# First quarter of a hybrid decoder trunk: a written start for embedding and first x, embeddings of quarter 1 moved behind the mixers, and delayed steps of the first heads

## The chip, the cores and the metric

The kernel runs on one core of a Trainium2 chip. The metric is the time of one execution on the device in microseconds (us), the median of several runs. The core has a matrix engine (TensorE, PE in the profile; its weight loads are PEld), a vector engine (VectorE, DVE), a scalar engine (ScalarE, ACT), GpSimd (POOL) and a queue engine (SyncE, SP), from which this kernel issues nearly all its DMA transfers. Each engine takes its own instructions in order, and semaphores tie them together.

## The reference

One layer of a decoder with 2048 tokens and 1024 channels, all in float32. Cut to what matters:

```
hn   = rms_norm(x, pre_mix_norm)
proj = hn @ w_in                                 # q,k,v,z,a,b of 4 DeltaNet heads; f,i,q,g of 4 HGRN2 heads
q, k, v = split(silu(causal_conv4(proj_qkv)))
o_a  = gated_delta_rule(l2norm(q), l2norm(k), v, decay(a), sigmoid(b)) -> head norm * silu(z)
o_b  = hgrn2(silu(q_hg), (1-lb)*sigmoid(-f), i_hg, log_f)              -> head norm * silu(g)
h = x + rms_norm(concat(o_a, o_b) @ w_out, post_mix_norm)
h = h + rms_norm(square(relu(rms_norm(h) @ w_up)) @ w_down)
e = rms_norm(p @ w_ple, ple_norm)
out = h + e * sigmoid(h @ w_gate)
```

The change touches the start (the scale of the first x, and p @ w_ple), the order of the two mixers in the first 512 tokens, and the end of the mixers' stage.

## The kernel before

Tokens are worked in four quarters of 512 (`QT`), channels as eight tiles of 128 (`KD`). A float32 product is made of three matmuls of a rounded high part and a low remainder: `split` (line 159) lets ACT write the high part and DVE subtract to get the low one; `operand` (197) does so for a 128x512 tile, after a scaling by a column and a row `rsb` where these are given; `project` (190) issues the three matmuls for each 128 channels. A tile of p @ w_ple has 256 input channels and so 6 matmuls; a block of `w_in` has 1024 and 24 matmuls.

**The start** (349 to 394). SP issues the loads in written order: half of `w_ple`, p of quarter 0, x of quarter 0 by rows (`xs`), small constants, p of quarter 1, the other half of `w_ple`, and x of quarter 0 again, transposed (`xraw`). ACT sums the squares of `xs` (375), POOL takes the power -1/2 (`rsqrt`, 157), and the 512 factors go through DRAM and back to a tile that holds them on all partitions (`spread` 228, `spread_load` 234). PE meanwhile makes 16 tiles of p @ w_ple, quarters 0 and 1 (`embed_tile`, 292): ACT copies each from PSUM and squares it, DVE adds the squares up, and the copy is stored to DRAM (`ed`). Then each of the eight x tiles is scaled and split (392). All this lives in a pool `es`; the mixers' pools `mp` and `m2` take the same room afterwards.

**The mixers' stage** (397 to 978). `works` (799) is a list of 4 x 33 products: for each quarter the decay columns (`mm_ab`) and, for each of four head pairs h, the eight blocks k, q, v, z (DeltaNet) and f, i, q, g (HGRN2). Each product is issued in three thirds of 8 matmuls, and after each third `tick` (344) advances a clock and runs the generators that are due: a head pair takes 24 ticks, a quarter 99. Head pair h of quarter 0 begins at tick t = 3 + 24 h.

`gdn_mixer` (534) is a generator of 39 steps whose offsets from t are `A_STEPS` (50). Counted from 0: step 2 transposes k, step 4 makes the matrices `u` and `qk`, steps 6 to 13 solve 32 rows of small triangular systems on DVE (`pr`, `xs_g`, lines 615 and 616), step 14 (offset 24) stores the result to DRAM, step 15 (26) loads it into `xx`, step 16 (28) transposes it on DVE, step 17 (30) begins the products on `xx` (`psp`, 638), steps 21 to 32 are the recurrence over four chunks (psa, `r` on DVE, psb, `w` on ACT, psc), step 33 on is the head norm. `hgrn_mixer` (681) and `turn_i` (782) have offsets of their own. `u`, `xx` and other tiles have one buffer, k and q (`conv_silu`, tags kT and qT) two.

PE's order is the written one throughout, and so is SP's in these stages; DVE, ACT and POOL are ordered by a planner, which goes by the written order and by which operands its model has ready.

**The end of the stage** (935 to 978). When the last product is issued, the last head pair still has some 20 ticks to go. In these, PE makes the 16 tiles of p @ w_ple of quarters 2 and 3 (one for each tick), whose p operands were loaded ahead (937), and then the first two blocks of the output product (`first_outs`, 949), 8 matmuls a tick. `mix_operands(0)` (313) loads and splits the mixers' result of quarter 0 meanwhile.

Of the kernel before, what the change touches and what calls it, by code (L numbers as in the profile page):

```python
# [20 lines left out]
P = 128  # L21
# [22 lines left out]
N_CONST = C_MASK + 2 * len(LEVELS)  # L44
# [16 lines left out]

def constants():
    j = np.arange(P)[:, None]
    i = np.arange(P)[None, :]
    c = np.zeros((P, N_CONST, P), np.float32)
    c[:, C_IDENT] = (i == j)
    c[:, C_NEG] = np.where(j <= i, 0.0, -1e30)
    c[:, C_UNIT] = (i % SB == GC * (j % GR) + i // SB)
    for n, s in enumerate(LEVELS):

        i = np.concatenate([m * P + np.arange(P).reshape(-1, 2, s)[:, 1].reshape(-1) for m in range(NC)])[None, :]
        m = (j // (2 * s) == i % P // (2 * s)) & (j % (2 * s) < s) | (s == 1) & (j == i % P)
        c[:, C_MASK + 2 * n : C_MASK + 2 * n + 2] = m.reshape(P, 2, P)
    return c
# [3 lines left out]
def trunk(ctx, tc, x, xT, pT, vecs, w_in, w_ab, gdn_a_log, gdn_dt_bias, w_out, w_up, w_down,  # L78
# [30 lines left out]
    mask = [cst[:, C_MASK + 2 * n : C_MASK + 2 * n + 2, :].rearrange("p a b -> p (a b)") for n in range(len(LEVELS))]  # L109
# [20 lines left out]
    def vectors():  # L130

        ps = bank("ps_rows", pp)
        PE.transpose(ps[:, :N_ROWS], rows, ident[:N_ROWS, :N_ROWS])
        V.tensor_copy(cols, ps[:, :N_ROWS])
        V.tensor_scalar(gate_w, cols[:, R_GNORM : R_HNORM + 1], 0.5, None, ALU.mult)
# [141 lines left out]
    def stage_ple(i, name):  # L277
# [5 lines left out]
        def ready(eng):  # L283
            w = wp.tile([P, 2, KD, P], F32R, tag="whl", name=f"w_{name}")
            for half in range(2):
                sl = slice(half * KD // 2, (half + 1) * KD // 2)
                split(w[:, :, sl], eng, raw[:, sl])
            return w
# [15 lines left out]
    x_r, xts, accs = {}, {0: []}, {0: None, 1: None}  # L304
# [44 lines left out]
    with ExitStack() as ectx:  # L349
        es = ectx.enter_context(tc.tile_pool(name="es", bufs=1))  # L350
        with tc.manual_schedule(engines={mybir.EngineType.SP}):
            ple0 = stage_ple(0, "plea0")
            praw = [es.tile([P, 2, QT], F32, name=f"praw{q}") for q in range(2)]
            nc.sync.dma_start(praw[0], pT[:, tok(0)].rearrange("(k p) t -> p k t", p=P))
            rows4 = x[tok(0), :].rearrange("(p c) d -> p c d", c=NC)
            xs = es.tile([P, NC, D], F32, name="xs")
            for c in range(0, NC, 2):
                nc.sync.dma_start(xs[:, c : c + 2], rows4[:, c : c + 2])
            nc.sync.dma_start(ident, consts[:, C_IDENT])
            nc.sync.dma_start(rows, vecs)  # L360
            nc.sync.dma_start(dec[:, 0:1], gdn_a_log.rearrange("o h -> h o"))
            nc.sync.dma_start(dec[:, 1:2], gdn_dt_bias.rearrange("o h -> h o"))
            nc.sync.dma_start(praw[1], pT[:, tok(1)].rearrange("(k p) t -> p k t", p=P))
            ple1 = stage_ple(1, "plea1")
# [6 lines left out]
            ple = [ple0(V), None]  # L371
            pts = [[operand(ra, None, f"pT{q}_{k}", raw=praw[q][:, k]) for k in range(2)] for q in range(1)]
            ss = sm.tile([P, NC], F32, tag="ss", name="ss_x0")
            for c in range(NC):
                S.activation(xs[:, c], xs[:, c], AF.Square, accum_out=ss[:, c : c + 1])
            V.tensor_scalar(ss, ss, 1.0 / D, EPS, ALU.mult, ALU.add)
            rsqrt(ss)
            stores = []
            for d in range(4):
                stores.append(embed_tile(0, d, ple[0], pts[0], accs, es, 6))  # L380
                if d == 1:
                    vectors()
            pts.append([operand(ra, None, f"pT1_{k}", raw=praw[1][:, k]) for k in range(2)])
            ple[1] = ple1(V)
# [1255 lines left out]
```

## Time and profile before

| | us |
|---|---|
| median of 3 runs | 2870.23 |
| lowest, highest | 2867.57, 2871.44 |
| profiled execution, its own time | 2865.62 |
| span of the profiled execution, first to last instruction | 2863.8 |
| PE busy in the span | 2773.0 (97%) |
| DVE busy | 2158.2 (75%) |
| ACT busy | 1331.2 (46%) |

The profile lists for each instruction its line, its tiles (out<-in), its start and length, and what ended the idle time of its engine before it. "x24" means 24 instructions merged in one row. Times inside the profile count from the first instruction. The granted clock (PEclk) is the share of full speed at which the matrix engine was allowed to run.

### The profile page before, as it was taken

The numbers are of one execution on the slowest core, as the hardware profiler recorded it, in microseconds if no ns is written. First come the engines' busy times: TensorE is split into PE (matmuls) and PEld (weight loads), VectorE is DVE, ScalarE is ACT, GpSimd is POOL, SyncE is SP. The second block draws the span as 40 slices with busy tenths as digits, with TensorE's granted clock in tenths as the row PEclk, the third lists the DMA queues.
The fourth block names the chain that finished last, engine by engine and source line by source line (L and its number), as shares of the span: only waits on it lengthen the run. The fifth ranks groups of instructions, "written<-read, shape, count | busy, mean of one in ns | idle before, by whom it ended". The sixth has DMA issues, their size and how long they took to land.

```text
span 2863.8 us, 39544 instructions
## 1 busy us (share of the span) xinstructions
PE 2773.0 (97%) x13361; PEld 2293.7 (80%) x13361; DVE 2158.2 (75%) x4712; ACT 1331.2 (46%) x2460; POOL 108.7 (4%) x104
## 2 busy tenths in 40 slices
PE   7899999999999999999989999999999999999999
PEld 5688788888888888777768887888888888887887
DVE  6688787887878887758887886776787765567675
ACT  6354334333333333457555655554555445465431
POOL 0000000000000000000000000000100000001000
PEclk9999999999999999999999999999999999999999
DMA  7666667655665666587755646666564446577573
GB/s 254 223 222 205 215 213 246 201 199 201 224 195 190 212 199 196 159 284 247 258 173 192 229 166 209 217 212 210 193 210 139 148 157 213 188 255 239 196 230 116
DMA packets 268602, 589.70 MB, mean 206 GB/s; under 512 B 55642, under 2 KB 59960, under 8 KB 249072
## 3 DMA queue, kind: packets, MB, share of 16 engines
q1 hardware_dynamic: 268400, 587.18, 61.5%
q8 instruction: 106, 1.74, 0.3%
q14 instruction: 96, 0.79, 0.1%
HBM read 420.14 MB, written 166.92 MB: 205 GB/s over the span
## 4 chain that ended last, share of the span: by engine, by line
PE 46%; DVE 3%; DMA 3%; issue 2%; ACT 2%; POOL 0%; SPq 0%; DVEq 0%; ACTq 0%; POOLq 0%
PE u L996 21%; PE d L996 18%; PE mmg L996 6%; DMA da<-sumd 1%; DMA raw_out<-in_w_out_dram 1%; DMA xo<-in_xT_dram 1%; DMA b<-h1d 0%; PE mmo L996 0%; DVE w_out L162 0%; DVE t L162 0%; ACT L1033 0%; ACT L1032 0%; ACT w_out L161 0%; DVE b L1143 0%; POOL acc_y L225 0%
## 5 line engine op out<-in xcount | busy, mean ns | idle before, releaser
L927 PE MATMUL mm<-xt,w 128*128 128x512 f32 x3072 | 791.2, 405 | 2.6 <-ACT w L161 1.2
L927 PEld LDWEIGHTS mm<-xt,w 128*128 128x128 f32 x3072 | 564.6, 191 | 122.8 <-ACT w L161 1.6
L996 PE MATMUL d<-db,da 128*128 128x512 f32 x2688 | 613.0, 390 | 4.2 <-DVE db L215 3.2
L996 PE MATMUL u<-t,wu 128*128 128x512 f32 x2604 | 603.4, 393 | 3.3 <-ACT wu L161 3.2
L996 PEld LDWEIGHTS d<-db,da 128*128 128x128 f32 x2688 | 504.0, 188 | 112.6 <-DVE db L215 5.8
L996 PEld LDWEIGHTS u<-t,wu 128*128 128x128 f32 x2604 | 488.8, 188 | 117.2 <-ACT wu L161 4.1
L215 DVE TENSOR_TENSOR db<-db 128x512 fp32r<-128x512 f32 x224 | 160.8, 718 | 69.9 <-ACT db L214 69.4
L1325 DVE TENSOR_TENSOR u<-u,u 128x512 f32<-128x512 f32 x224 | 150.8, 684 | 72.1 <-PE u L996 71.0
L996 PE MATMUL mmo<-mixT,w_out 128*128 128x512 f32 x720 | 171.5, 398 | 9.1 <-DVE w_out L162 6.8
L214 ACT ACTIVATE db<-db 128x512 fp32r<-128x512 f32 x224 | 140.9, 629 | 78.7 <-DMA db<-hid 76.3
L996 PE MATMUL mmg<-h2T,wg 128*128 128x512 f32 x768 | 177.5, 393 | 0.0
L996 PEld LDWEIGHTS mmo<-mixT,w_out 128*128 128x128 f32 x720 | 137.0, 191 | 42.6 <-DVE w_out L162 8.5
L996 PEld LDWEIGHTS mmg<-h2T,wg 128*128 128x128 f32 x768 | 144.2, 188 | 32.8
L1366 ACT ACTIVATE u<-u 128x512 f32<-128x512 f32 x128 | 80.9, 632 | 179.6 <-DVE u L1325 179.2
L162 DVE TENSOR_TENSOR da<-da 128x512 fp32r<-128x512 f32 x128 | 94.3, 737 | 91.0 <-ACT da L161 90.5
L615 DVE TENSOR_TENSOR pr_g<-xs_g,sys_g 128x4 f32<-128x4 f32 (+30 forms) x496 | 136.1, 274 | 29.3 <-DMA sys_g<-ud_g 19.3
L161 ACT ACTIVATE da<-da 128x512 fp32r<-128x512 f32 x128 | 80.5, 629 | 140.0 <-DMA da<-sumd 117.3
L616 DVE TENSOR_REDUCE xs_g<-pr_g 128x4 f32<-128x8 f32 (+30 forms) x496 | 111.0, 224 | 9.8
L161 ACT ACTIVATE wu<-a 128x512 fp32r<-128x512 f32 x124 | 73.9, 622 | 46.7 <-DMA a<-in_w_up_dram 44.6
L225 POOL TENSOR_TENSOR acc_y<-acc_y,sq_y 128x512 f32<-128x512 f32 x28 | 38.7, 1382 | 1389.4 <-ACT sq_y L224 1389.4
L162 DVE TENSOR_TENSOR wu<-a,wu 128x512 fp32r<-128x512 f32 x124 | 84.9, 688 | 4.0 <-ACT wu L161 4.0
L726 PE MATMUL at_h<-q_h,k_h 128*128 128x64 f32 x640 | 82.6, 273 | 3.2 <-DVE tail_g L548 1.7
(364 smaller groups left out, 3893.1 us busy)
## 6 DMA issues: line engine op xcount, KB each, us to landing
w<-cache_in SPq DMA_DIRECT2D x96, 1024.0 KB
db<-hid SPq DMA_DIRECT2D x224, 256.0 KB
cache_in<-w SPq DMA_DIRECT2D x32, 1024.0 KB
hid<-u SPq DMA_DIRECT2D x128, 256.0 KB
da<-sumd SPq DMA_DIRECT2D x128, 256.0 KB
a<-in_w_up_dram SPq DMA_DIRECT2D x124, 256.0 KB
hid<-ht SPq DMA_DIRECT2D x96, 256.0 KB
dr<-in_w_down_dram SPq DMA_DIRECT2D x96, 256.0 KB
```

Of the source, the lines that this page charges most:

```text
L161: S.activation(t[:, 0], raw, AF.Copy)
L162: eng.tensor_tensor(t[:, 1], raw, t[:, 0], ALU.subtract)
L214: S.activation(t[:, 0], plain(t), AF.Copy)
L215: V.tensor_tensor(t[:, 1], plain(t), t[:, 0], ALU.subtract)
L225: eng.tensor_tensor(acc, acc, sq, ALU.add)
L615: V.tensor_tensor(pr[:, :, 0:i], xs[:, :, 0:i], sys[:, None, 0:i, i].broadcast_to([P, GC, i]), ALU.mult)
L616: V.tensor_reduce(xs[:, :, i], pr[:, :, 0 : i + 1], AX.X, ALU.add)
L726: PE.matmul(ps[:, c, :], k[:, blk(c)], odd, start=True, stop=True)
L927: PE.matmul(ps, *terms[i], start=i == 0, stop=i == nt - 1)
L996: PE.matmul(ps, a, b, start=start, stop=stop)
L1325: V.tensor_tensor(c[new], c[old], ps, ALU.add)
L1366: S.activation(c[k], c[k], AF.Relu)
```

## The change

- **Loads.** x by rows and p of quarter 1 are no longer loaded at the start. The transposed x comes right after p of quarter 0. The masks of the HGRN2 levels shrink from 14 tiles of 128x128 to 4, are read with a broadcast over the four chunks, and are loaded after the eight x operands.
- **Scale of the first x.** ACT squares `xraw`, two tiles at a time, DVE adds up, four small matmuls against ones give the sums as columns, POOL takes the root, DVE multiplies it into a diagonal, and one float32 matmul of ones with the diagonal puts the factors on all partitions in PSUM. The way through DRAM goes.
- **Order.** In this block DVE and ACT run in the written order, as SP and PE do. The scale of tile k+1 is written ahead of the split of tile k. The weights of `mm_ab` are split inside the block, and those of the first k product are loaded there.
- **Embeddings.** Only the 8 tiles of quarter 0 are made at the start; the sums of their squares are added at the end of the block. Those of quarter 1 go to the end of the mixers' stage, ahead of those of quarters 2 and 3; there p of the next quarter is loaded when tile 6 of a quarter is issued (`load_p`).
- **Delays.** In quarter 0, head pair 0 does its steps from 14 on 6 ticks later, pair 1 its steps from 4 on 4 ticks later, pair 2 those from 4 on 2 ticks later. k and q get a third buffer. One step of `decays` is a tick later in quarter 0. `mix_operands(0)` and the second output block come some 8 ticks later.

```diff
+A_FIRST = ((14, 6), (4, 4), (4, 2), (0, 0))
...
-    mask = [cst[:, C_MASK + 2 * n : C_MASK + 2 * n + 2, :].rearrange("p a b -> p (a b)") for n in range(len(LEVELS))]
+    mask = [cst[:, C_MASK + n // 2, n % 2 * (P // 2) : (n % 2 + 1) * (P // 2)] for n in range(len(LEVELS))]
...
-        with tc.manual_schedule(engines={mybir.EngineType.SP}):
+        first = {mybir.EngineType.SP, mybir.EngineType.Activation, mybir.EngineType.DVE}
+        with tc.manual_schedule(engines=first):
             ple0 = stage_ple(0, "plea0")
-            praw = [es.tile([P, 2, QT], F32, name=f"praw{q}") for q in range(2)]
-            nc.sync.dma_start(praw[0], pT[:, tok(0)].rearrange("(k p) t -> p k t", p=P))
-            rows4 = x[tok(0), :].rearrange("(p c) d -> p c d", c=NC)
-            xs = es.tile([P, NC, D], F32, name="xs")
-            for c in range(0, NC, 2):
-                nc.sync.dma_start(xs[:, c : c + 2], rows4[:, c : c + 2])
...
-            nc.sync.dma_start(praw[1], pT[:, tok(1)].rearrange("(k p) t -> p k t", p=P))
+            praw = es.tile([P, 2, QT], F32, name="praw0")
+            nc.sync.dma_start(praw, pT[:, tok(0)].rearrange("(k p) t -> p k t", p=P))
             xraw = es.tile([P, KD, QT], F32, name="xraw")
...
+            ple1 = stage_ple(1, "plea1")
+            ab_ready = stage("ab0", w_ab)
...
+            ple[0] = ple0(V, lambda: pt.extend(operand(ra, None, f"pT0_{k}", raw=praw[:, k]) for k in range(2)))
+            homes = (pm, pm, pp, pp, pm, pm, pp, pp)
...
+            def put(d):
+                if d % 2 == 0:
+                    es_sq[d // 2] = es.tile([P, 2, QT], F32, name=f"esq{d // 2}")
+                e = es.tile([P, QT], F32, tag="ld", name=f"e0_{d}", bufs=KD)
+                S.activation(e, sums[d], AF.Copy)
+                S.activation(es_sq[d // 2][:, d % 2], sums.pop(d), AF.Square)
+                puts.append((ed[0][d], e))
...
+            def x_squares(k):
+                if k == 0:
+                    S.activation(total, xraw[:, :2], AF.Square)
+                else:
+                    sq = es.tile([P, 2, QT], F32, tag="xsq", name=f"xsq{k}", bufs=2)
+                    S.activation(sq, xraw[:, k : k + 2], AF.Square)
+                    V.tensor_tensor(total, total, sq, ALU.add)
+
+            embed(0)
+            x_squares(0)
+            embed(1)
+            put(0)
+            x_squares(2)
+            embed(2)
+            x_squares(4)
+            put(1)
+            embed(3)
+            x_squares(6)
+            acc = st.tile([P, QT], F32, tag="acc", name="acc_x0", bufs=3)
+            V.tensor_tensor(acc, total[:, 0], total[:, 1], ALU.add)
+
+            columns_of_rows()
+            ps = bank("ss_x0", po)
+            for c in range(NC):
+                PE.matmul(ps[:, c : c + 1], acc[:, blk(c)], one[:, 0:1], start=True, stop=True)
+            ss = sm.tile([P, NC], F32, tag="ss", name="ss_x0")
+            V.tensor_scalar(ss, ps[:, :NC], 1.0 / D, EPS, ALU.mult, ALU.add)
+            rsqrt(ss)
+            ple[1] = ple1(V)
+            put(2)
+            diag = es.tile([P, NC, P], F32, name="xdiag")
+            V.tensor_tensor(diag, over_chunks(ident), ss[:, :, None].broadcast_to([P, NC, P]), ALU.mult)
+            rsb = bank("rs_x0", po)
+            embed(4)
+            PE.matmul(rsb, one, diag.rearrange("p c n -> p (c n)"), start=True, stop=True)
+            put(3)
+            split_w = {0: ab_ready()}
+            w0_ready = stage("4_0_0", w_in[4])
+            for d in range(5, KD):
+                embed(d)
...
+            scaled(0)
+            for k in range(KD):
+                scaled(k + 1)
+                xts[0].append(operand(ra, None, f"xt0_{k}", raw=raws[k]))
+                if k in (1, 3, 5, 6):
+                    put({1: 4, 3: 5, 5: 6, 6: 7}[k])
             nc.sync.dma_start(cst[:, C_NEG:], consts[:, C_NEG:])
...
+            for a in puts:
+                nc.sync.dma_start(*a)
+            vectors()
+            pair = es_sq[0]
+            for i in range(1, KD // 2):
+                V.tensor_tensor(pair, pair, es_sq[i], ALU.add)
+            accs[0] = st.tile([P, QT], F32, tag="acc", name="acc_e0", bufs=3)
+            V.tensor_tensor(accs[0], pair[:, 0], pair[:, 1], ALU.add)
...
-            g["k"] = conv_silu(ps, 4 + h, f"kg{q}_{h}", "kT", 2)
+            g["k"] = conv_silu(ps, 4 + h, f"kg{q}_{h}", "kT", 3)
...
+                if q == 0:
+                    step, by = A_FIRST[h]
+                    a_steps = a_steps[:step] + tuple(o + by for o in a_steps[step:])
                 at(t, gdn_mixer(q, h, g), a_steps)
...
-                            at(clock[0], decays(ps, q), (0, 2, 4, 5))
+                            at(clock[0], decays(ps, q), (0, 2, 5, 6) if q == 0 else (0, 2, 4, 5))
...
-            qs = (2, 3)
+            qs = (1, 2, 3)
...
-            at(clock[0], mix_operands(0), (1, 2, 3, 4, 6, 7, 9, 11))
+            at(clock[0], mix_operands(0), (9, 10, 11, 12, 14, 15, 18, 19))
...
-            call(clock[0] + 13, partial(ready_out, 1))
-            call(clock[0] + 14, partial(stage_out, 2))
+            call(clock[0] + 21, partial(ready_out, 1))
+            call(clock[0] + 22, partial(stage_out, 2))
...
-            while clock[0] <= last or len(held) < 2 or 1 in ready:
+            while clock[0] <= last or fill or len(held) < 2 or 1 in ready:
                 if fill:
...
+                    if d == KD - 2 and q + 1 in qs:
+                        store()
+                        store = None
+                        pts[q + 1] = load_p(q + 1)
```

More of the change, by code (lines that the diff above doesn't have):

```diff
@@ L287, in ready, with stage @@
                 split(w[:, :, sl], eng, raw[:, sl])
+                if half == 0 and then is not None:
+                    then()
+            return w
+        return ready
+    def stage(name, src, k=KD):
+        raw = wp.tile([P, k, P], F32, tag="raw", name=f"raw_{name}", bufs=2)
+        nc.sync.dma_start(raw, src)
+        def ready():
+            w = wp.tile([P, 2, k, P], F32R, tag="whl", name=f"w_{name}")
+            split(w, V, raw)
             return w
@@ L823, in trunk @@
         last = t + LAST
-        staged, split_w = {}, {}
+        staged = {1: w0_ready}
         def stage_work(j):
```

84 lines of the change are left out of this document (30 added, 54 removed).

## The prediction

> **What bounds the kernel now.** I read first the busy times in stretches cut at the borders of the stages: the start up to the first product of the mixers, the four quarters, and the end of the mixers' stage. The columns are the stretch, its length, the busy time of PE, PEld, DVE, ACT and POOL, the granted clock, the DMA share and GB/s.
>
> ```profile
> 0.00:46.09 46.09, 28.87 (x98) 19.52 (x98) 27.29 (x54) 32.57 (x60) 1.23 (x5) 0.93 0.83 299
> 46.09:328.15 282.06, 261.72 (x1386) 219.90 (x1387) 224.86 (x644) 123.51 (x258) 16.11 (x14) 0.97 0.65 215
> 328.15:610.49 282.34, 278.03 (x1559) 237.11 (x1558) 230.59 (x709) 102.74 (x242) 15.59 (x17) 0.99 0.66 220
> ...
> 1179.30:1245.56 66.26, 58.89 (x326) 49.47 (x324) 46.11 (x100) 38.76 (x71) 5.49 (x5) 0.97 0.64 210
> ```
>
> PE is the bound: quarter 1 leaves it idle for 4.3 us of 282. Three stretches that the change touches leave more: the start 17.2 us, quarter 0 20.3 us, the end of the stage 7.4 us. So a matmul that is only moved costs its time wherever PE lands it, and what can be won is idle time. Next, what PE waited for, over the whole span (total, times, longest):
>
> ```profile
> PE psp_g L638 <- DVE xx_g L630: 17.6, 4, 10.6
> PE psb_g L667 <- DVE r_g L664: 14.1, 20, 1.3
> ```
>
> The longest wait for a producer in the mixers is one of 10.6 us, and the sequence in time (below) puts it in quarter 0. I make the sum against the profiled execution: 2865.62 us, of which the span is 2863.8 and 1.8 lie around it. It ran 4.6 us under the median of 2870.23; I carry the difference over to the median.
>
> **The start.** What matters is when the mixers' pools may be touched: they take the room of `es`, and everything in them waits for its last reader.
>
> ```profile
> 7.06 1.15 ACT L161 ACTIVATE pT<-praw 128x512 fp32r<-128x512 f32 x2 [1.00 <-DMA praw<-in_pT_dram]
> 13.08 1.06 ACT L375 ACTIVATE xs<-xs 128x1024 f32<-128x1024 f32 x1
> 15.16 0.60 ACT L224 ACTIVATE sq_e<-mme 128x512 f32<-128x512 f32 x1
> 15.55 1.02 POOL L157 TENSOR_TENSOR ss_x<-ss_x,mhalf 128x4 f32<-128x4 f32 x1 [15.11 <-DVE ss_x L376]
> 26.09 1.23 DVE L162 TENSOR_TENSOR w_ab<-raw_ab,w_ab 128x1024 fp32r<-128x1024 f32 x1 [2.70 <-ACT w_ab L161]
> 28.02 2.08 DVE L203 SCALAR_TENSOR_TENSOR xraw<-xraw,cols,rsb_x 128x512 f32<-128x512 f32 x3 [0.71 <-DMA rsb_x<-rd_x]
> 30.02 1.29 DVE L162 TENSOR_TENSOR xt<-xraw,xt 128x512 fp32r<-128x512 f32 x2
> 51.38 0.53 POOL L624 MEMSET xx_g<- 128x512 f32 x1 [34.80 <-DMA ed<-e]
> 115.03 0.59 PE L711 MATMUL at_h_d<-att_h,one 128*128 128x256 f32 x2
> 115.47 1.05 PE L714 MATMUL at_h<-hb_h,k_h 128*128 128x128 f32 x8
> ```
>
> Before, the last reader is a store of `ed`: POOL and DVE first touch the mixers' room at 51.38. After, I add up the written order. ACT is free at 7.06 for p (1.15); then come half a weight split (0.58), four squarings of 128x1024 (1.06 each) and two puts (two passes of 0.60 each): 7.06 + 1.15 + 0.58 + 4.24 + 2.40 = 15.4. The x loads don't hold this up: the same 2 MB stood at the same place of the queue before, and their last piece was squared from 13.08, so it would be done at 14.1. Then DVE's add of 1024 columns (1.23) and of 512 (0.69, from L203) make 17.3. The four float32 matmuls against ones are two records each, and none in this trace has one column; I bound them by the eight records of L714 above (1.05) and by nothing, and take 1.05, since the weight load is the same: 18.4. Scale and root, a small DVE operation and POOL's 1.02 with the hand-overs, are 1.3: 19.7. The diagonal, 0.69: 20.4. The float32 matmul of 512 columns isn't in the trace; two records of 256 take 0.59, so it lies between that and twice that, and as columns set a matmul's length I take 1.2: 21.6. The second `w_ple` split (two subtracts) and that of `mm_ab` fall into the gaps in which DVE waits for POOL and PE. From there DVE sets the pace: eight scales of 0.69 and eight subtracts of 0.65 are 10.7, and ACT's first copy (0.58) stands ahead of the first subtract: 32.9. `vectors` has some ten small operations (0.17 each) and a trip to ACT and back, 2.2; the sums of squares are three adds of 1.23 and one of 0.69, 4.4: release at 39.5, or 40.7 if the planner slips the first k weights' subtract (1.22) in ahead. I take 40.4 against 51.38, **11.0 us earlier**. What follows, zeroing, decays and the first convolution, is the same DVE work in the same order. The bounds: 8 us, if written order costs a stall of a third of a microsecond at each of the eight tiles, and 13, if the squarings are not held up by the puts and end with the loads at 14.1.
>
> The stores of `ed` no longer matter there: the last tile is copied by ACT about 33. The load of the constants from C_NEG on and the first k weights go ahead of them on SP, but they are early. PE's first product and `mm_ab` run before 40 and lie under DVE's chain.
>
> **The moved tiles.** Eight tiles of quarter 1 leave the start, where their time is already in the 11 us, and are paid at the end of the stage.
>
> ```profile
> 1194.66 1.66 PE L188 MATMUL mme<-pT,w_pleb 128*128 128x512 f32 x6 [0.42 <-ACT sq_e L224]
> 1196.04 0.43 SPq L317 DMA_DIRECT2D mixT<-mixd  x1
> 1199.20 0.38 SPq L299 DMA_DIRECT2D ed<-e  x1
> 1200.50 0.63 ACT L214 ACTIVATE mixT<-mixT 128x512 fp32r<-128x512 f32 x1 [2.63 <-DMA mixT<-mixd]
> 1201.31 0.60 ACT L297 ACTIVATE e<-mme 128x512 f32<-128x512 f32 x1 [0.19 <-DMA ed<-e]
> 1205.43 2.57 PE L188 MATMUL mme<-pT,w_pleb 128*128 128x512 f32 x6
> 1224.24 1.64 PE L188 MATMUL mme<-pT,w_pleb 128*128 128x512 f32 x6
> 1226.31 1.65 PE L188 MATMUL mme<-pT,w_pleb 128*128 128x512 f32 x6
> 1228.02 1.67 PE L188 MATMUL mme<-pT,w_pleb 128*128 128x512 f32 x6
> ```
>
> From 1226.31 to 1228.02 lie a tile and one psa, so a tile is some 1.48 us net; eight are **11.8 us later**. The bound below: they fill all 7.4 us of idle time here and cost 4.4. I take the full price, as the last head's chain has the same number of ticks and the added tiles come where its ticks are nearly over.
>
> **The new wait for p.** `load_p` takes two tiles of a tag with two buffers, which also holds the copies of the tiles. So at the change of quarter stands a chain: tile 6 copied (0.60), stored, its buffer free (1199.20 to 1201.31 above: 2.1), p loaded (1196.04 to 1200.50: 4.5 in a busy stretch, 2.1 if as short as the store), split on ACT and DVE (0.63 + 0.65): 6.1 to 8.5 us from the end of tile 6 to the first tile of the next quarter. SP stands still for the store, and what is behind it waits too. At the first change, tile 6 ends at 1196.3 and the ninth tile began at 1205.43 anyway, held by waits of the last head: hidden, if those waits stay. At the second, tile 6 ends at 1225.9 and the next quarter's tile stands at 1228.02: 4.0 to 6.4 us bare. I take 4.0 less half a microsecond of later waits that this covers: **3.5 us**. Bounds: 0, if the planner's order lets p come early, and 8.7, if the first change is bare by 2.3 too.
>
> **The delays.** The wait in quarter 0 and its neighbours:
>
> ```profile
> 116.28 5.85 PE L927 MATMUL mm<-xt,w 128*128 128x512 f32 x24
> ...
> 132.77 2.05 PE L638 MATMUL psp_g<-xx_g,um 128*128 128x128 f32 x8 [10.65 <-DVE xx_g L630]
> 134.61 1.81 PE L726 MATMUL at_h<-q_h,k_h 128*128 128x64 f32 x8
> 136.18 2.69 PE L927 MATMUL mm<-xt,w 128*128 128x512 f32 x8
> ...
> 142.78 1.00 PE L726 MATMUL at_h<-q_h,k_h 128*128 128x64 f32 x8
> 147.41 1.05 PE L638 MATMUL psp_g<-xx_g,um 128*128 128x128 f32 x8
> ```
> ```profile
> 127.72 0.32 SPq L620 DMA_DIRECT2D xd_g<-xs_g  x1
> 132.31 0.89 DVE L630 STREAM_TRANSPOSE xx_g<-xx_g 128x128 f32<-128x128 f32 x4 [2.86 <-DMA xx_g<-xd_g]
> ```
> ```profile
> 130.00:140.00 10.00, 7.23 (x32) 6.62 (x33) 2.93 (x10) 2.19 (x7) 0.00 (x0) 0.63 0.80 260
> ...
> sum 50.00, PE 37.66 PEld 31.31 DVE 38.20 ACT 19.90 POOL 1.01; mean PE 7.53 PEld 6.26 DVE 7.64 ACT 3.98 POOL 0.20
> ```
>
> PE stands 10.65 us for the transposes of head 0. The store of the solution waits at the front of SP's queue until 127.72, and the weights that are written behind it wait too. Afterwards the clock is 0.63, and three groups take 2.05, 1.81 and 2.69 instead of 1.05, 1.00 and some 2.1 (a third of the 24 in 5.85, and the tail of a matmul): 2.4 us more. Six ticks put 48 matmuls, 2 x 5.85 = 11.7 us, ahead of the wait, and the store leaves the front of SP's queue; so the wait goes, 13.05 us with the clock. What is late next is DVE: from 100 to 150 it has 38.2 us of work, and 50 - 38.2 = 11.8 is all that this stretch can shrink. I take **11.8 us**, and 0.6 for the decays' transposes, which waited 0.61 and come a tick later. Bounds: 6.6 us, if a wait of head 1 to 3 grows by what the longest other one in this quarter costs, 3.17 us and 1.2 of clock as at 318.29 in the next row, and 17.4, if that one goes with the first (13.05 + 4.4).
>
> ```profile
> 318.29 0.77 PE L748 MATMUL pso_h<-q_h,S_h 128*128 128x128 f32 x2 [3.17 <-DVE S_h L747]
> ```
>
> Buffers: the recurrence of pair n now ends in the tick in which pair n+1 clears `xx`, two ticks closer than before; that tick and the next three cover POOL's 0.53 and the load of some 3 us. The third k and q buffer takes away what the delay would add. Masks, constants and the later loads of mixed tiles I cost at nothing: the broadcast has the same element count, and the loads lie under tiles that have no other DMA but their own stores.
>
> **The sum**: -11.0 + 11.8 + 3.5 - 11.8 - 0.6 = -8.1 us: 2857.5 for the profiled execution, 2862 for the median.
>
> **The rivals.**
> 1. Larger gain: the moved tiles fill the idle time of the end (4.4 instead of 11.8), and p costs nothing, with the rest as forecast: -19, 2851. For it: 7.4 us idle in 66. Against it: the tiles come last, the idle time first.
> 2. The delay doesn't do what it says: DVE, given the same work and fewer us, brings `xx` six ticks later too, and 11.8 fall away: +3.7, 2874. Against it: DVE idled 2.86 us just there for the load.
> 3. Clock: each new halt of PE is followed by slow matmuls as after 132.77, 2.4 us. Two are new, at the release near 40 and at the second change of p: +4.8, 2867. For it: 0.63 after the wait of 10.65; against it: ahead of the release PE has a product paced by DVE, not a full halt.
>    [...]
> 4. Slower: the delayed recurrences. Three heads have four chunks each, in each of which psb waits for `r` from DVE. In quarter 0 DVE is busy 224.86 of 282, and the delay packs the heads' chains closer. If each of the 12 waits 1.3 us, the longest seen, that is 15.6: +7.5, 2878. It decides from 0.7 us for each. Against it: the 20 that wait in the whole trace have 0.7 on average, and most of 64 don't.
>
> **How the numbers follow.** Forecast 0.40 (2855 to 2867), larger gain 0.25 (down to 2844), no effect of the delay 0.08, clock 0.11, slower 0.16. What a measurement of this kernel can tell from no change is about 0.2%, 5.7 us. Faster: 0.33 of the forecast, 0.25 and 0.04 of the clock case, 0.62. Slower: 0.16 and 0.02 of case 2, 0.18. The rest, 0.20, is no change. The range, 2846 to 2877, leaves out the tail of case 1 and half of case 4.
>
> **What would show it.** First touch of the mixers' room (zeroing on DVE) near 40 instead of 51.4; no wait for `xx` over 3 us in quarter 0, and that quarter (first `mm_ab` matmul to the next) near 270 with the start near 25; the end of the stage near 81 us, with a wait for p's split at the second change. The prediction is wrong if release comes after 46, if a wait of the same size stands six ticks later, or if the waits for `r` in quarter 0 sum to over 8 us.

## The result, and the profile after

The changed kernel takes 2887.07 us (median of 4 runs, 2885.06 to 2888.75) beside 2870.84 of the kernel before on the same chip (4 runs): a ratio of 1.0062, 95% interval 1.0050 to 1.0075. It is slower, by 17.8 us by the ratio (0.0062 of 2865) and 16.2 by the two medians, where the prediction had 8 us faster. The profiled execution took 2885.06 us with a span of 2883.3, 19.5 more than before.

First the busy times of the changed kernel in stretches: the start up to the first q product, the four quarters, and the end of the mixers' stage (columns as in the prediction: stretch, length, busy PE, PEld, DVE, ACT, POOL, granted clock, DMA share, GB/s).

```profile
0.00:45.31 45.31, 30.74 (x108) 22.12 (x108) 32.08 (x63) 27.37 (x46) 2.14 (x6) 0.92 0.70 243
45.31:317.75 272.44, 253.70 (x1329) 212.12 (x1329) 214.20 (x621) 117.35 (x247) 12.13 (x12) 0.96 0.64 212
317.75:607.60 289.85, 282.55 (x1567) 241.02 (x1566) 231.60 (x713) 102.47 (x243) 16.71 (x17) 0.98 0.66 215
607.60:890.83 283.23, 275.38 (x1559) 234.90 (x1558) 226.55 (x701) 102.69 (x242) 15.66 (x17) 1.00 0.61 205
890.83:1173.54 282.71, 275.19 (x1560) 234.70 (x1558) 225.93 (x701) 95.72 (x224) 14.64 (x16) 1.00 0.57 188
1173.54:1263.68 90.14, 74.83 (x375) 60.29 (x374) 54.28 (x112) 50.36 (x94) 7.78 (x7) 0.92 0.56 182
```

Against the same marks before, this adds up to the whole difference of the two spans, 19.5 us:

| stretch | before | after | difference |
|---|---|---|---|
| start, to the first q product | 57.97 | 45.31 | -12.7 |
| quarter 0 from there | 270.18 | 272.44 | +2.3 |
| quarter 1 | 282.34 | 289.85 | +7.5 |
| quarters 2 and 3 | 568.81 | 565.94 | -2.9 |
| end of the mixers' stage | 66.26 | 90.14 | +23.9 |
| all the rest | 1618.2 | 1619.6 | +1.4 |

The start and the release of the mixers' room came as worked out. From the sequence in time of the changed kernel:

```profile
17.24 1.51 PE L429 MATMUL ss_x<-one,acc_x 128*128 128x1 f32 x8 [2.37 <-DVE acc_x L424]
21.49 1.91 PE L439 MATMUL rs_x<-xdiag,one 128*128 128x512 f32 x2
41.81 0.09 DVE L480 MEMSET bound<- 128x36 f32 x1
```

The first touch of the room stands at 41.81, where 40.4 was forecast and 51.4 was before.

What PE waited for in quarter 0 (total, times, longest), before and then after:

```profile
PE psp_g L638 <- DVE xx_g L630: 10.6, 1, 10.6
PE pso_h L748 <- DVE S_h L747: 3.2, 1, 3.2
PE at_h L726 <- DVE tail_g L548: 1.7, 1, 1.7
```
```profile
PE at_h L785 <- DVE k_h L788: 4.1, 2, 3.8
PE nrm_g L267 <- DVE hl_g L167: 4.0, 2, 2.3
PE mm L985 <- ACT gb L513: 4.0, 1, 4.0
PE psp_g L697 <- DVE xx_g L689: 3.9, 1, 3.9
PE psb_g L726 <- DVE r_g L723: 2.1, 4, 1.4
```

The wait of 10.6 us is gone. In its place stand several of 1 to 4 us, nearly all for DVE (the one for gb lies just ahead of the first q product at 45.31), and quarter 0 is no shorter. At the end of the stage the new waits are these, PE's own and what holds the operand back:

```profile
1201.31 0.50 PE L193 MATMUL mme<-pT,w_pleb 128*128 128x512 f32 x1 [1.38 <-ACT pT L166]
...
1222.32 1.97 SPq L318 DMA_DIRECT2D ed<-e  x2
1225.53 0.97 SPq L206 DMA_DIRECT2D raw_pT<-in_pT_dram  x2
1228.99 0.63 ACT L166 ACTIVATE pT<-raw_pT 128x512 fp32r<-128x512 f32 x1 [5.49 <-DMA raw_pT<-in_pT_dram]
1229.68 2.80 PE L193 MATMUL mme<-pT,w_pleb 128*128 128x512 f32 x5 [6.80 <-ACT pT L166]
...
1242.83 0.63 ACT L219 ACTIVATE mixT<-mixT 128x512 fp32r<-128x512 f32 x1 [2.53 <-DMA mixT<-mixd]
1245.43 2.09 PE L193 MATMUL mme<-pT,w_pleb 128*128 128x512 f32 x6 [3.27 <-ACT sq_e L229]
```

Here the reader sees the chain that `load_p` makes: the stores of the last two copies, then p's load, then the split, and PE standing for 6.80 us. Of the 23.9 us, 7.9 are idle time of PE (15.3 against 7.4) and 15.9 busy time: eight tiles of 1.48, and a rest of some 4 us that goes with the lower granted clock (0.92 against 0.97).

### The profile page after: what moved, and what is told of

Its sections match the earlier page's. It is cut to its first block, busy times and chain, and to the rows that moved or that the text cites. A ratio compares the mean times of both kernels' runs of the same rounds, so it can differ in the third digit from the quotient of the medians.

```text
span 2883.3 us, 39566 instructions
## 1 busy us (share of the span) xinstructions
PE 2784.0 (97%) x13371; PEld 2299.7 (80%) x13371; DVE 2159.2 (75%) x4714; ACT 1328.0 (46%) x2456; POOL 108.7 (4%) x104
## 4 chain that ended last, share of the span: by engine, by line
PE 46%; DVE 3%; issue 3%; DMA 3%; ACT 2%; POOL 0%; SPq 0%; DVEq 0%; ACTq 0%; POOLq 0%
PE u L1062 21%; PE d L1062 18%; PE mmg L1062 6%; PE mmo L1062 1%; DMA da<-sumd 1%; DMA raw_out<-in_w_out_dram 0%; DMA xo<-in_xT_dram 0%; DVE w_out L167 0%; DMA b<-h1d 0%; DVE t L167 0%; ACT L1099 0%; DVE acc_o L230 0%; DVE b L1209 0%; DVE yo L1132 0%; ACT L1098 0%
## 5 line engine op out<-in xcount | busy, mean ns | idle before, releaser
L785 PEld LDWEIGHTS at_h<-q_h,k_h 128*128 128x128 f32 x640 | 80.5, 197 | 10.8 <-issue 7.1
```

The costliest lines, as they stand in the source:

```text
L785: PE.matmul(ps[:, c, :], k[:, blk(c)], odd, start=True, stop=True)
```

## The experiments

All ratios are to the kernel before on the same chip, with their 95% intervals; the last column is the ratio's distance from 1, times 2865 us. Differences between runs below are differences of that column. The intervals are 3 to 4 us wide to either side, so a difference of two runs is known to some 5 us (an estimate, by the root of the sum of the squares). e5, e6, e13, e14 and e15 leave out work that the output needs, so they are measurements and no candidates.

| run | ratio | interval | us |
|---|---|---|---|
| the change | 1.0062 | 1.0050 to 1.0075 | +17.8 |
| e1 without the delays | 1.0050 | 1.0035 to 1.0065 | +14.3 |
| e2 e1, p loaded earlier | 1.0028 | 1.0018 to 1.0038 | +8.0 |
| e3 before, with the delays | 1.0009 | 0.9998 to 1.0020 | +2.6 |
| e4 e1, tiles in quarter 0 | 1.0060 | 1.0045 to 1.0075 | +17.2 |
| e5 e1, no tiles of quarter 1 | 0.9964 | 0.9952 to 0.9977 | -10.3 |
| e6 e5, with the delays | 0.9965 | 0.9952 to 0.9978 | -10.0 |
| e7 e4, tiles two products earlier | 1.0039 | 1.0027 to 1.0051 | +11.2 |
| e8 e7, tiles' sums on GpSimd | 1.0041 | 1.0026 to 1.0056 | +11.7 |
| e9 before, low parts on GpSimd | 1.0043 | 1.0028 to 1.0058 | +12.3 |
| e10 e9, with the delays | 1.0066 | 1.0051 to 1.0081 | +18.9 |
| e11 written start with 16 tiles | 1.0013 | 1.0003 to 1.0023 | +3.7 |
| e12 e11, low parts on GpSimd | 1.0064 | 1.0049 to 1.0079 | +18.3 |
| e13 before, low parts left out | 0.9965 | 0.9953 to 0.9978 | -10.0 |
| e14 e13, with the delays | 0.9960 | 0.9944 to 0.9975 | -11.5 |
| e15 before, no tiles of quarter 1 | 0.9968 | 0.9956 to 0.9979 | -9.2 |

### The delays: e1, e3, e6

```diff
-A_FIRST = ((14, 6), (4, 4), (4, 2), (0, 0))
+A_FIRST = ((0, 0), (0, 0), (0, 0), (0, 0))
```

> The changed kernel with the delays of quarter 0 set to zero, all else kept. Theory A (the loss sits at the end of the mixers' stage; the delays only spread one long wait over several short ones): the wait for xx of some 10 us is back in quarter 0, the short waits there are gone, and the time stays within 4 us of the changed kernel's 2887. Theory B (the delays themselves cost, in quarter 0 and by what they leave to quarter 1): 6 to 10 us faster than the changed kernel, 2877 to 2881. The prediction's step (the delays win 11.8 us): 10 us or more slower than the changed kernel.

> The kernel before with the delays alone (with the third k and q buffer and the small masks that make room for it). Theory A: within 4 us of the kernel before. Theory B: 5 to 10 us slower. The prediction's step: the wait of 10.65 us is gone with nothing in its place, 10 to 12 us faster.

e1 undoes the delays in the changed kernel; e3 puts them, with the small masks and the third k and q buffer, into the kernel before. In both, theory A holds (within 4 us). Without the delays the wait is back, and longer; this is PE in e1:

```profile
122.07 1.20 PE L697 MATMUL psp_g<-xx_g,um 128*128 128x128 f32 x4 [12.76 <-DVE xx_g L689]
```

In the profiles the delays make quarter 0 shorter by 4.3 us in the changed kernel (276.7 in e1, 272.4 with them), not by 11.8; in e3 it is 3.4 us longer than before (285.4 against 282.1, from `mm_ab` to `mm_ab`). In the ratios nothing is left: the change is 3.4 us over e1, e3 2.6 us over before, and e6, the cleanest pair, is 0.3 us over e5. With some 3 to 6 us of uncertainty on each, the delays bring nothing that shows, and a gain of 11.8 us is ruled out by all three.

> The run e5 with the delays put back: nothing but the delays differs. Theory A (the delays trade one wait of 12.75 us for several short waits for VectorE, and lose in quarter 1 what they win in quarter 0): 0 to 8 us slower than e5, with waits of 2 to 4 us for k_h, r, xx and hl in quarter 0. Rival (the delays are worth their 11.8 us and the new end hides it): 8 to 12 us faster than e5.

It came out at the edge of theory A, with waits of the size that it named for k_h (3.5 us), xx (3.9) and hl (2.3), and a shorter one for r (1.3). What became of DVE's idle time is in these stretches of quarter 0: e1 from its first q product, then e5 and e6 from 45 us, each to the next `mm_ab`.

```profile
44.68:321.40 276.72, 253.53 (x1336) 212.62 (x1337) 217.97 (x626) 117.46 (x248) 12.96 (x12) 0.95 0.62 209
45.00:320.07 275.07, 252.27 (x1336) 211.51 (x1337) 218.35 (x627) 119.11 (x250) 12.97 (x12) 0.95 0.62 211
45.00:316.11 271.11, 252.38 (x1329) 210.90 (x1329) 214.61 (x622) 118.26 (x248) 12.14 (x12) 0.97 0.63 213
```

DVE is idle for 58.7 us in e1 and 58.2 in the changed kernel (272.44 - 214.20), for 56.7 in e5 and 56.5 in e6. So the delays use up none of DVE's idle time over the quarter. The quarter gets shorter by 4.3 and 4.0 us, and DVE is busy for 3.8 and 3.7 us less in it. The delays change no work, only its place, so the quarter is shorter by about the DVE work that now falls behind its end. In the 50 us around the wait alone (90 to 140) DVE's idle time does fall, from 13.0 in e1 to 7.3; it comes back elsewhere in the quarter.

e6 against e5 also says that the long quarter 1 of the changed kernel (289.85) doesn't belong to the delays as such: with the same delays e6's quarter 1 takes 281.8, and in e1 and e3 it takes 280.8 and 284.4. In the changed kernel short waits of 0.5 to 2.2 us are followed there by stretches of low clock (0.73 from 340 to 350, 0.83 from 370 to 380 and from 430 to 440), but its waits are 7 us in all and e6's 5, and why the quarter is 8 us longer stays open.

### The moved tiles: e5, e15, e2

e5 is e1 with the old end of the stage and without quarter 1's tiles:

```diff
-            qs = (1, 2, 3)
+            qs = (2, 3)
...
```

> After the change without the delays, with the old end of the stage, and with quarter 1's eight embeddings left out altogether (its output is made with the embeddings of quarter 0). Theory A (the new end costs far more than the prediction's 11.8 + 3.5 us: 27 us in the profile of the run without delays, from the first embedding tile to the end): 2880.7 - 27 = 2854, between 2850 and 2858. Rival (the end costs 15 us, the rest of the loss lies in the mixers' quarters): 2865, over 2861.

It is 24.6 us faster than e1, and e6 is 27.8 us faster than the change. So the eight tiles and the new end of the stage that they need cost 25 to 28 us, each to some 5 us, where 11.8 + 3.5 were forecast. In the profiles the end of the stage takes 91.2 us in e1 and 68.8 in e5, 22.4 less.

e15 leaves the same tiles and their p out of the old start:

```diff
...
-            for d, q in [(d, 1) for d in range(4)] + [(d, q) for d in range(4, KD) for q in range(2)]:
-                stores.append(embed_tile(q, d, ple[d // 4], pts[q], accs, es, 6))
-                stores.pop(0)()
+            for d in range(4, KD + 4):
+                if d < KD:
+                    stores.append(embed_tile(0, d, ple[d // 4], pts[0], accs, es, 6))
+                if stores:
+                    stores.pop(0)()
...
```

> The kernel before with quarter 1's eight embeddings and their p left out of the old start (its output is made with the embeddings of quarter 0), all else as before. If the gain of the start (e5, 10.3 us) comes from the eight tiles that left it, this run has it too: 8 to 11 us below before. If it comes from the new way of the scale and the written order: 0 to 4 us below before, and e5 stays faster by 6 us or more.

```profile
40.12 0.09 DVE L409 MEMSET bound<- 128x36 f32 x1
```

The old start without the tiles lets go of the room at 40.12, earlier than the new one (41.81), and the time falls by 9.2 us, beside 10.3 with the new start. The gain of the start is the tiles' leaving it; the diagonal, the dropped loads and the written order add 1.1 us, which the intervals don't tell from nothing.

e2 is e1 with p loaded three tiles earlier, into two buffers of its own (k and q go back to two buffers for it, in e2 and also in e4, e7, e8, e11 and e12):

```diff
...
-                    if d == KD - 2 and q + 1 in qs:
-                        store()
-                        store = None
+                    if d == KD - 5 and q + 1 in qs:
                         pts[q + 1] = load_p(q + 1)
```

> As e1_no_delay, with p of the next quarter loaded three tiles earlier into two buffers of its own, so that no store of a tile stands before it (k and q have two buffers, to make room). Theory A (the end of the stage waits for p at both changes of quarter): the two waits of PE for p, 1.4 and 6.8 us in the changed kernel, are gone, the end of the stage shrinks from 90 to about 80 us, and the time is 8 to 11 us under e1_no_delay. Rival (the last head's chain or ACT would hold PE there anyway): the waits move to other producers, less than 3 us under e1_no_delay.

PE no longer waits for p at the end of the stage, and 6.3 us are won (14.3 to 8.0), between the 8 of theory A and the 3 of the rival; the end takes 84.8 us in the profile, 6.4 less than in e1. But the time still lies 18.3 us over e5. What is late next are ACT's copies, behind stores that free the copies' two buffers, and behind loads of the mixers' result:

```profile
1216.03 1.22 PE L193 MATMUL mme<-pT,w_pleb 128*128 128x512 f32 x2 [1.83 <-ACT sq_e L229]
...
1224.01 1.20 PE L193 MATMUL mme<-pT,w_pleb 128*128 128x512 f32 x4 [2.18 <-ACT sq_e L229]
...
1236.41 0.79 PE L193 MATMUL mme<-pT,w_pleb 128*128 128x512 f32 x1 [3.06 <-ACT sq_e L229]
```

So of the 24.6 us, 11.8 are the tiles, 6.3 the wait for p, and 6.5 are left over (24.6 - 11.8 - 6.3). In the profiles of the end alone 4.2 are left over (22.4 - 11.8 - 6.4). That this rest is the waits above and the clock (0.66 in e2 from 1215 to 1220 and from 1235 to 1240, 1.00 in the other stretches of 5 us from 1170 to 1240) is argued from the trace; no run takes them away.

### Other places for the tiles: e4, e7, e8, e11

e4 and e7 put the tiles into quarter 0, as products that take no tick; e7 puts them two products earlier. e8 is e7 with the tiles' sums and low parts on GpSimd.

```diff
...
+        for i in range(2):
+            works.insert(11 + i, (f"plef{i}", "ple", None, 0, i, None, None, None))
...
+                if key == "ple":
+                    embed_half(h, split_w.pop(j))
+                    continue
...
```

> The written start of the changed kernel, no delays, the end of the stage as before the change, and the 8 tiles of quarter 1 issued as two products without ticks right ahead of the third product of the second head pair, where PE of the kernel before waits 10.65 us for xx. Theory A (start 9.6 us earlier, a moved matmul is free only where PE waits): 8 to 13 us under the kernel before, 2858 to 2863, with the wait for xx mostly filled. Rival (DVE sets the pace in quarter 0, so the wait only moves behind the tiles): 2 us under it to 4 us over it.

e4 missed both of its forecasts (17.2 us over before). PE stood for 19.22 us in place of 12.76:

```profile
125.32 1.06 ACT L166 ACTIVATE w<-raw 128x1024 fp32r<-128x1024 f32 x1 [8.17 <-DMA raw<-in_w_in_dram]
...
134.01 1.22 PE L193 MATMUL mme<-pT,w_plef 128*128 128x512 f32 x2 [19.22 <-ACT acc_e L907]
```

The copies of the tiles stood in ACT's order behind this weight and behind further loads (they start at 132.90), and SP loads the weight behind the store of the solution, which goes out at 117.11: the filler hung on the queue that the wait had blocked.

> As e4, with the eight embeddings of quarter 1 put two products earlier, ahead of the place where SyncE stands for the store of head pair 0's solution. Theory A (in e4 the copies of the tiles stood in ScalarE's order behind weights that SyncE could not load; here they don't): no wait of 19 us, the tiles take the place of the 12.75 us wait, 2880.7 - 27 = 2854, up to 2858. Rival (VectorE's work ahead of xx sets the time, and the tiles' sums and splits, some 9.6 us, come on top of it): a wait for xx of 8 us or more stays, 2862 to 2868.

> As e7, with the low parts of the moved weights and of p, and the sums of the squares, made by GpSimd instead of VectorE. If VectorE's work sets the time of xx: 4 to 10 us faster than e7. If not: the same as e7 within 2 us. If GpSimd is slow at it or holds VectorE up: slower than e7, with waits of VectorE or TensorE for GpSimd in quarter 0.

e7 fills the wait of head pair 0 (0.70 us of it is left), and it doesn't help (11.2 us over before, where neither theory had more than 6): other waits come, and quarter 0 takes 290 us (45.33 to 335.56) beside 274 in e5 (46.07 to 320.07), which is more than the tiles' 11.8.

```profile
107.86 1.22 PE L193 MATMUL mme<-pT,w_plef 128*128 128x512 f32 x2 [4.74 <-ACT sq_e L910]
...
274.95 1.44 PE L698 MATMUL psp_g<-xx_g,um 128*128 128x128 f32 x5 [8.37 <-DVE xx_g L690]
...
327.48 0.79 PE L727 MATMUL psb_g<-r_g,xx_g 128*128 128x128 f32 x2 [5.11 <-DVE r_g L724]
```

e8 is the same as e7; as in e9 below, where GpSimd subtracts, an operation of DVE takes up to 2.49 us in place of 0.42, that doesn't settle whether DVE's work sets the time there. e11 keeps all 16 tiles in the written start:

```diff
...
+            praw1 = es.tile([P, 2, QT], F32, name="praw1")
+            pt1 = [es.tile([P, 2, QT], F32R, name=f"pT1_{k}") for k in range(2)]
...
+            for d in range(KD):
+                embed1(d)
...
```

> The written start without delays, with the eight embeddings of quarter 1 kept in the start (p of quarter 1 loaded there, sums of squares on GpSimd) and the old end of the stage. In e5, TensorE stood for some 15 us of the first 45, so if the start has room for them, the tiles cost less than 11.8: the first q product goes from 45 to 48 or 51, and the time is 4 to 8 us below before. If TensorE, ScalarE and SyncE have no room there: 11.8 us or more over e5, the same as before or slower.

It is 14 us over e5 (3.7 + 10.3) and no faster than before: the first q product waits until 61.73. Of the four new places that were tried for the tiles, none is cheaper than their own 11.8 us of PE: 14.0 here, 21.5 in e7, 24.6 at the end (e1) and 27.5 in e4, each against e5. In the old start they cost 9.2 (before against e15), which isn't told from 11.8, but it is the cheapest place on record. No version with all of the work in it beat the kernel before.

### Does VectorE set the pace of quarter 0? e9, e10, e12, e13, e14

e9 moves 31 subtracts of quarter 0's weights from DVE to GpSimd, in the kernel before; e12 does so in e11.

```diff
-                split(w, V, raw)
+                split(w, V if name in ("ab0", "4_0_0") else G, raw)
```

> The kernel before with one edit: in quarter 0 the low parts of the weights (one subtract of 1.22 us a product on VectorE) are made by GpSimd, where 512 columns took 1.31 us in e8, so some 2.6 us a product. Theory A (VectorE's work sets the pace of quarter 0): head pair 0's solution comes up to eight subtracts, 9.8 us, earlier, the wait of 10.65 us for xx shrinks to 1 to 4 us and the time falls by 8 to 14 us. Rival (the order of the transfers or the latency of the chain sets the pace): within 3 us of before, the wait for xx still over 7 us. If GpSimd's subtracts come late for TensorE: slower, with waits for w from GpSimd.

It was slower, and no test: DVE was not relieved (busy for 243.9 us of quarter 0, against 224.9 before, though it does 31 subtracts less). The wait for xx is 7.7 us. Groups of instructions in e9 from 60 to 330 us (form, count, busy us, mean ns):

```profile
L162 POOL TENSOR_TENSOR w<-raw,w 128x1024 fp32r<-128x1024 f32 x29 | 71.5, 2464 | 154.0 <-ACT w L161 154.0
```
```profile
L729 DVE TENSOR_TENSOR k_h<-k_h,gg_h 128x256 f32<-128x256 f32 x18 | 13.6, 755 | 0.0
L696 DVE TENSOR_TENSOR gg_h<-f_h 128x256 f32<-128x256 f32 x4 | 7.6, 1901 | 0.0
```

and the same two of DVE in the kernel before:

```profile
L729 DVE TENSOR_TENSOR k_h<-k_h,gg_h 128x256 f32<-128x256 f32 x18 | 7.6, 420 | 0.0
L696 DVE TENSOR_TENSOR gg_h<-f_h 128x256 f32<-128x256 f32 x4 | 1.7, 420 | 0.0
```

> e9 with the delays of the change (as e3, with the low parts of quarter 0's weights on GpSimd). Theory A (in e3 the delays only moved the wait, as VectorE had no time to spare): with VectorE relieved of 39 us in quarter 0 the delays can take away what is left of the waits for VectorE, 2 to 8 us faster than e9. Rival (the delays pack the head pairs' chains, and waits for r, hl and xx come whatever VectorE has to do): the same as e9 within 2 us, or slower.

> e11 with the low parts of quarter 0's weights on GpSimd (from the second product on). If the two gains lie in different stretches, they add up: e11's difference to before plus e9's. If GpSimd, which has the sums of squares of the start as well, comes late: less than the better of the two.

e10 and e12, which carry the same edit, lost too (6.6 us over e9, 14.6 over e11).

e13 takes the subtracts off DVE with GpSimd idle:

```diff
-                split(w, V, raw)
+                if name == "ab0":
+                    split(w, V, raw)
+                else:
+                    for p in range(2):
+                        S.activation(w[:, p], raw, AF.Copy)
```

> The kernel before, but in quarter 0 ScalarE writes the second half of each weight tile too (a second rounded copy, 1.06 us a product; the low part itself is left out, so the products of quarter 0 and those made with the kept weights are less exact), and VectorE has 31 subtracts of 1.22 us less, with GpSimd idle. Theory A (VectorE's work sets the pace of quarter 0): the wait of 10.65 us for xx shrinks to 1 to 4 us, quarter 0 gets 10 to 16 us shorter, ratio 0.994 to 0.997. Rival (the serial chain of head pair 0 or the transfers set the pace): the wait stays over 7 us, ratio 0.998 to 1.001.

```profile
127.01 1.17 PE L642 MATMUL psp_g<-xx_g,um 128*128 128x128 f32 x8 [4.34 <-DVE xx_g L634]
```

The wait for xx falls from 10.65 to 4.34 and the time by 10.0 us, with DVE busy for 194.3 us of quarter 0 in place of 224.9: DVE's work does set the pace of that wait. It doesn't set all of it: the wait stays above the 1 to 4 us that were expected, and in the profile the quarter gets 6.0 us shorter (282.1 to 276.0), not 10 to 16.

> e13 with the delays of the change. Theory A: with VectorE relieved the delays no longer run into short waits for k_h, r, xx and hl, and win what is left of the wait for xx: 2 to 8 us faster than e13. Rival (packing the chains of the head pairs costs what it wins, whatever VectorE has to do): within 2 us of e13, or slower.

```profile
PE mm L938 <- ACT hist L505: 4.1, 2, 3.0
PE nrm_g L265 <- DVE hl_g L165: 1.8, 2, 1.4
...
PE psp_g L645 <- DVE xx_g L637: 0.4, 1, 0.4
```

With DVE relieved, the delays take away what is left of the wait (0.4 of 4.3), the waits that came in its place are shorter than in the changed kernel, and quarter 0 is shorter by some 3.6 us from the release on (49.27 to 322.07 in e13, 48.19 to 317.41 in e14). By the ratios that is 1.4 us, which isn't told from nothing and fits the rival. DVE's idle time is the same again (78.6 us in e13 and 77.9 in e14, from 55 us to the next `mm_ab`). That the short waits shrink is shown; that the delays then pay is not.

## Why the prediction was wrong

The forecast was 8.1 us faster, the measurement is 17.8 us slower. Along the runs e5, e6 and the change, 12.7 of these 25.9 us are the delays with the 0.6 of the decays, 12.5 the end of the stage, and 0.7 the start; along e5, e1 and the change the delays have 15.8 and the end 9.3. Two steps failed, then, by about as much each.

**The start** (-11.0) was right: the room is free 9.6 us earlier in the profile, and e5 is 10.3 us faster. Its chain was worked out along the new order, and the trace keeps to it: the sums at 17.24 where 17.3 was worked out, the release at 41.81 where 40.4 was. But the text didn't see that nearly all of the gain would be had without that order (9.2 us in e15). Two of its terms came out longer: the four small matmuls took 1.51 us in place of 1.05 and the one of 512 columns 1.91 in place of 1.2, at granted clocks of 0.64 and 0.50. That columns set a matmul's length was the author's estimate, and the trace before shows it only in part: two records of 256 columns take 0.59, but eight of 64 take 1.00, as long as eight of 128 (1.05).

**The moved tiles and the wait for p** (+11.8 and +3.5) were right in kind and too small: 24.6 to 27.8 us. The tiles' own 11.8, an estimate from the trace before, was not tested apart. The wait at the second change was priced at the lower end of its range, less what later waits cover, 3.5; in the trace the chain from the end of tile 6 (1220.3) to the next quarter's tile (1229.68) takes 9.4 us, where 6.1 to 8.5 were worked out, and by e2 the waits for p cost 6.3. Some 4 to 6.5 us are left for which the prediction had no term: it cost the loads of the mixers' result "at nothing" and gave ACT's copies no price, and in the trace ACT takes these copies late, behind the mixers' result and the stores, and the first matmuls after the stop of 6.80 us ran at a lower clock (the granted clock is 0.52 from 1229.68 to 1232.91, where six of them take 3.23 us, and 1.00 from 1220.29 to 1221.94, where six take 1.65). The share of each is not shown.

**The delays** (-11.8, and -0.6 for the decays) are the step that failed in its mechanism. The prediction worked out "11.8 is all that this stretch can shrink" from DVE's 38.2 busy us of 50, and took this bound as the value. The runs show that DVE's idle time over the quarter stays as it was (58.7 and 58.2 us, 56.7 and 56.5). The wait of 10.65 us went, as said; its time came back as waits for k_h, hl and xx. Why DVE can't spend its idle time there is argued, not shown: it too waits for products, transfers and ACT, and the work that the delay pushes on meets it later. Measured: 0.3 us lost (e6), 2.6 and 3.4 lost (e3, e1), none told from nothing. The decays' 0.6 didn't come either: the wait of 0.61 for gb is 1.54 in the changed kernel.

By these sizes the sum is -10.3 + 27.8 + 0.3 = 17.8 us. It meets the measured loss by construction, since the three are differences along a chain of runs (before, e5, e6, the change); it is no further test.

**The rivals.** The second (DVE brings xx later too, and the 11.8 fall away) was nearest, with a chance of 0.08: its size is right, though the wait moved to other places and didn't reappear at its own. The larger gain fell with the end of the stage: no idle time there took the tiles. The clock was right in kind, at the end above all (0.97 to 0.92): both halts that it named came (3.98 and 6.80 us), and the matmuls after them are slow (the clock is 0.72 in the first 5.4 us after 45.31, where 16 take 5.39 us, and 1.00 from 53.37, where 16 take 4.00; the six after 1229.68 are given above), some 3 us in all by these rows, where 4.8 were worked out. The rival on the slower side, the waits for r, fell: in quarter 0 they are 2.1 us together, and in the whole span 15.3 against 14.1.

**What was to show it.** Release near 40: yes. No wait for xx over 3 us in quarter 0: one of 3.93. The quarter from `mm_ab` to `mm_ab` near 270 from a start near 25: 289.8 (27.98 to 317.75). These two marks didn't fit the prediction's own sum, which puts the quarter's end at 304.8 (328.15 - 11.0 - 11.8 - 0.6) and not at 295; it came 10.4 us earlier than before, which is the gain of the start alone. The end near 81: 90.14, with the wait for p where it was expected. None of the three signs of being wrong came (release after 46, a wait of the same size six ticks later, over 8 us for r): they watched for the old wait coming back whole, and not for DVE's idle time staying or for an end over 81.

## What to carry to other kernels

A stretch's idle time on the next engine in line is a bound on what removing a wait can bring, not its value: where that engine serves many short chains, the wait can come back in pieces, as here; so look for the change that takes work off it (e13) rather than one that shifts the work (e3, e6, e7). Work that left one stage was paid in full or more at each of the four new places here, and with it came the transfers, the copies on the other engines and the buffers that it needed there; price these as terms. To know what a rewritten stage is worth, take out of the old one what was moved away, before crediting the rewriting.

## What the runs showed of the hardware

**Work on DVE took longer beside a subtract on GpSimd.** In e9 a row of the triangular solve takes 2.43 us instead of some 0.23 beside a subtract on GpSimd, and the two end within 0.1 us of each other (109.97 and 110.06):

```profile
107.44 2.53 POOL L162 TENSOR_TENSOR w<-raw,w 128x1024 fp32r<-128x1024 f32 x1 [7.21 <-ACT w L161]
107.63 2.43 DVE L615 TENSOR_TENSOR pr_g<-xs_g,sys_g 128x40 f32<-128x40 f32 x1
110.33 0.24 DVE L615 TENSOR_TENSOR pr_g<-xs_g,sys_g 128x44 f32<-128x44 f32 x1
```

In the same run a product of 128x256 on DVE (L696) that took 415 to 422 ns before took up to 2485 ns, about the whole 2.46 us of one subtract on GpSimd, while the convolution's instructions (L496), which read a product from PSUM, kept their time (means of 0.72 to 0.75 us, 0.74 to 0.75 before). Instructions with one input took longer too: from 60 to 330 us the two TENSOR_SCALAR of 128x4 on `m_h` (L270) take 2.00 us on average and the two on `m_e` 1.21, where those of the kernel before take 0.15 to 0.17. Why some operations took longer and others didn't is not shown by these runs.

**The clock fell after short waits too.** In the changed kernel, waits of 0.90 and 2.29 us before 269 and of 1.76 and 3.93 before 199.5 are each followed by a stretch at a reduced clock (0.66 from 270 to 280, 0.73 from 200 to 210). A single wait of 2.09 before 371.75 is too (0.66 from 372 to 374, 0.50 from 374 to 376). Not all are: after waits of 1.14 and 1.40 before 178.5 and 182.2 the granted clock stays at 1.00 up to 195. The sequence in time, then the windows:

```profile
195.06 0.50 PE L267 MATMUL nrm_g<-hl_g,ones 128*128 128x512 f32 x1 [1.76 <-DVE hl_g L167]
...
199.48 2.08 PE L697 MATMUL psp_g<-xx_g,um 128*128 128x128 f32 x8 [3.93 <-DVE xx_g L689]
...
266.16 0.49 PE L266 MATMUL nrm_g<-hl_g,ones 128*128 128x512 f32 x1 [0.90 <-ACT hl_g L166]
...
268.94 0.50 PE L267 MATMUL nrm_g<-hl_g,ones 128*128 128x512 f32 x1 [2.29 <-DVE hl_g L167]
```
```profile
200.00:210.00 10.00, 10.00 (x52) 9.03 (x51) 3.47 (x7) 2.72 (x4) 0.00 (x0) 0.73 0.54 205
...
270.00:280.00 10.00, 10.00 (x46) 8.66 (x46) 7.42 (x22) 5.23 (x18) 1.01 (x1) 0.66 0.48 164
```

By my estimate from these two windows, in which PE is busy throughout, that is 2.7 and 3.4 us lost (0.27 and 0.34 of 10), beside 5.7 and 3.2 us of waiting. With several short waits in place of one long one, this price was paid more than once in the changed kernel's quarter 0.
